# The order of three kinds of matrix product in a scheduled encoder layer: 16-bit products ahead of float32 ones, and a longer hold for the inverse steps of the early blocks

## The chip, the cores and the metric

The kernel runs on one core of a Trainium2 chip. The metric is the device time of one execution in microseconds (us); lower is better. The time before is the median of three runs, 2339.23 us (2339.19 to 2341.5).

## What is computed

One layer of a streaming encoder for 2048 frames of a new stream and 64 frames of a running one, model width 1024, all in float32:

```python
h = rmsnorm(x, norm1_w);  proj = h @ w_in          # q, k, v, z, a, b, u_pool
# (A) gated delta rule, 4 heads of 128, chunked; per chunk and head:
T = inverse(eye + Lm)                              # Lm: strictly lower triangular
u = T @ (v * beta);  w = T @ (k * beta * exp(G))
v_new = u - w @ S;  o = (q * exp(G)) @ S + qk @ v_new;  S = S * d_last + k_tail.T @ v_new
# (B) trailing means over 2/4/8/16 frames, minus the frame, one 128x128 map per group
x = x + concat(o_delta, o_pool) @ w_out
h = rmsnorm(x, norm2_w);  x = x + (silu(h @ w_gate) * (h @ w_up)) @ w_down
y = rmsnorm(x, normf_w)
```

## The kernel before, in words

**Kinds of product.** Tokens lie along the free dimension. The large products (projection `pp`, output projection `pz`, gate and up `px`/`py`/`pz`, down `d`/`dx`/`dy`/`dz`) are made of float32r products: weight and activation are each split into a high and a low part, and three products (high-high, high-low, low-high) are added in PSUM. The program calls these kind "r". Transposes and plain float32 products are kind "f": `ptk`, `ptv` (transposes of keys and values), `gr` (key and query Gram matrices), and the serial state recurrence `pk` and `po`. 16-bit products are kind "h": the triangular inverse (`py`, `pt` by level 0 to 6, then `pf` and `px_p`) and half of the decay mask (`gb`). A plain float32 product on 128 columns stands in the trace as two matmuls, a transpose and a 16-bit product as one.

**Stages.** The mixer runs over four blocks of 512 tokens (block 0 also carries the 64 frames of the running stream). For each block j: projections `pp` of one head after another (`head_project`), four heads of delta rule in the background, the pooling groups, the norm of the next block; the output projection `pz` of block j-1 stands after the second head of block j. The operand tiles h of a block have one buffer, so the next block's h can only be written once the last `pp` of this one has read them; the output projection of block 2 reads its operand from tiles in that same place, filled from DRAM (`op<-od`), after the last `pp` of block 3. The output projection of block 3 comes last, with its pooling half first and its head half second. Then the feed-forward part runs over three token blocks in Strassen form, with float32r products nearly alone.

**A delta-rule head.** Each head has two fronts of two 128-token chunks. A front goes `ptk`, `gb`, `gr`, then levels `py` (TensorE) - mask (VectorE) - `pt` (TensorE) - copy (ScalarE, `TV_p<-pt_p`) - next `py`, and so on to `pf`, `px_p`, `ptv`. The recurrence then goes chunk by chunk through `pk` and `po`, and ends in a norm (`os`), from which the head's operand of the output projection is written (`op<-osq`). Every second step of these chains is on another engine, so TensorE does other work in between.

**What sets the order.** Nothing is issued as it is written. The kernel records every operation (`Machine.note`, which is why every instruction carries line 278), and `Machine.issue` then plays the whole program through once with a cost for each operation and hands the instructions to each engine in the order that comes out. An operation has a rank: its place in the recording, less a boost. The delta-rule chains run with `BOOST` = 100000, so their ranks are negative. On the other engines the ready operation of lowest rank goes first. On TensorE, `Machine.pick` decides: if any ready product is not of kind r, the one of lowest rank is taken, unless the last product was of kind r, another r is ready, and each waiting product has been ready for less than its `HOLD`: 0.4 us of the planner's clock for negative ranks, 3.0 for others. So a run of r products is broken when one other product has waited long enough, and then all the ready others go together before the r products go on.

Of the kernel before, what the change touches and what calls it, by code (L numbers as in the profile page):

```python
# [58 lines left out]
class Machine:  # L59
# [6 lines left out]
    def __init__(self, nc):  # L66
        self.nc, self.ops, self.seen, self.boost, self.n = nc, [], {}, 0, 0
        self.tiles, self.slots, self.queue, self.parked, self.later, self.early = {}, {}, {}, {}, {}, 0
        self.free = {e: 0.0 for e in ("tensor", "vector", "scalar", "gpsimd", "sync")}
        self.last, self.at = None, 0.0  # L70
        self.busy = {"vector": 0.0, "gpsimd": 0.0}
        self.wire = 0.0
        self.gone = 0.0
        for e in self.free:
            setattr(self, e, Engine(self, e))
# [205 lines left out]
    def pick(self, ready, t):  # L281

        others = sorted(x for x in ready if x[2].kind != "r")
        if others:
            first = others[0]
            held = self.last == "r" and len(others) < len(ready) and t < min(x[2].ready + HOLD[x[0] >= 0] for x in others)
            if held:
                first = min(x for x in ready if x[2].kind == "r")
            ready.remove(first)
            heapq.heapify(ready)  # L290
            return first[2]
        return heapq.heappop(ready)[2]

    def run(self, op, t):
        op.start = t
        if op.eng == "tensor":

            free, kind = self.free["tensor"], op.kind
            if self.last == kind and op.ready <= free:
                op.start = max(t, self.at + op.ldw)  # L300
            elif kind == "r":
                if op.ready <= free:
                    op.start = max(op.ready, free - (0.028 if self.last == "h" else 0.081))
                op.occ, op.lat = op.occ + 0.087, op.lat + 0.087
            elif self.last == "h":
                op.occ, op.lat = op.occ + 0.054, op.lat + 0.054
            else:
                op.occ, op.lat = op.occ + 0.02, op.lat + 0.02
            self.at, self.last = op.start, kind
            self.free["tensor"] = op.start + op.occ  # L310
        elif op.eng == "sync":
            self.free["sync"] = t + op.occ
            self.wire = max(self.wire, t + op.occ) + op.size / (
                (STORE if op.store else 400e3) if op.size > 300000 else 320e3)
            op.lat = self.wire + 1.35 - t
        else:
            if op.port:

                other = "gpsimd" if op.eng == "vector" else "vector"
                more = min(max(self.busy[other] - t, 0.0), op.occ)  # L320
                op.occ, op.lat = op.occ + more, op.lat + more
                self.busy[op.eng] = t + op.occ
            self.free[op.eng] = t + op.occ
# [32 lines left out]
def hybrid_kernel(ctx, tc, a, o):  # L356
# [61 lines left out]
    def drain(until=lambda: False):  # L418
        while chains and not until():
            c = min((c for c in chains if c.runnable()), key=lambda c: c.at)  # L420
            if c.at > clock["pe"]:
                clock["lost"] = clock.get("lost", 0) + c.at - clock["pe"]
                clock["pe"] = c.at
            c.step()
# [93 lines left out]
    ready, due, stored = [], [], set()  # L518
# [264 lines left out]
    def project(B, *ms):  # L783

        ws = [weights("win", m) for m in ms]

        out = [[bank(("ok", (1, 2))[m][i], f"pp{m}_{i}") if B.j == 0 and m < 2 else psmm(f"pp{B.j}_{m}_{lo}")
                for i, (lo, n) in enumerate(B.subs)] for m in ms]
        for ks in (range(4), range(4, KT)) if len(ms) > 1 else (range(KT),):
            for m, w, pss in zip(ms, ws, out):  # L790
                for (lo, n), ps in zip(B.subs, pss):
                    for k in ks:
                        one_k(B, m, w[k // 4], ps[:, :n], k, slice(lo, lo + n))
                        pump()
        return out if len(ms) > 1 else out[0]
# [469 lines left out]
    def fold_pool():  # L1265

        for g in range(4):
            ts(poolw[:, g, :], poolw[:, g, :], psc[:, g : g + 1], None, ALU.mult)
            for i in range(2):
                t = wpool.tile([P, 512], F32, tag="xs", name=f"fw{g}_{i}", bufs=XBUFS["xs"])  # L1270
                sl = slice(4 * i, 4 * i + 4)
                t3 = t.rearrange("p (m c) -> p m c", c=P)
                nc.sync.dma_start(out=t3, in_=a["wout"][sl, :, (4 + g) * P : (5 + g) * P].rearrange("m p c -> p m c"))
                yield 4.0
                ps = psg(f"fp{g}_{i}")
                mm(ps, poolw[:, g, :], t, start=True, stop=True)
                nc.scalar.copy(t, ps)
                nc.sync.dma_start(out=wpd[sl, :, g * P : (g + 1) * P].rearrange("m p c -> p m c"), in_=t3)
                yield LAT_APPLY

    def new_o(B, pool=None, tag="op", bufs=2):
        four = [(pool or opool).tile([P, 4, 2, MB], F32R, tag=tag or f"h{k}", name=f"op{k}_{B.j}", bufs=bufs) for k in range(2)]
        B.o, B.o4 = [four[k // 4][:, k % 4] for k in range(KT)], four[0]

    def pools(B):
        for gs in ((0,), (1,), (2,), (3,)) if B.dec else ((0,), (1,), (2, 3)):
            pps = project(B, *(17 + g for g in gs))
            for g, pp in zip(gs, pps if len(gs) > 1 else (pps,)):
                B.pools.append(Chain(pool_group(B, g, pp)))

    def out_proj(B):
        acts = [(k, B.o[k]) for k in (4, 5, 6, 7, 0, 1, 2, 3)]

        late = [0] if B.kept else []
        src = stream_x(a["xT"], "xc", B.t0, "xc")
        for ms in ((0, 1), *((m,) for m in range(2, KT))) if B.kept else ((m,) for m in range(KT)):
            ws = [weights("wout", m, *late) for m in ms]
            for lo, n in B.subs:
                xs = [src(m, lo, n) for m in ms]
                pss = [psmm(f"pz{B.j}_{m}_{lo}") for m in ms]  # L1300
                for part in (acts[:4], acts[4:]) if len(ms) > 1 else (acts,):
                    for w, ps in zip(ws, pss):
                        dense(ps, w, part, lo, n, first=part[0] is acts[0], last=part[-1] is acts[-1])
                for m, x, ps in zip(ms, xs, pss):
                    add_x(B, m, x, ps[:, :n], lo)
# [66 lines left out]
    for j in range(NBLK):  # L1372
        first = None
        if j:
            pab, first = project(B, 0, 1)
        else:
            pab = project(B, 0)
        machine.boost = HOT_ROWS
        rows(B, pab)
        machine.boost = 0  # L1380
        blocks.append(B)
        nxt = Block(j + 1) if j + 1 < NBLK else None
        B.heads, B.pools = [], []
        if prev is None or nxt is None:
            new_o(B)
        for h in range(NH):
            B.heads += head_project(B, h, first if h == 0 else None)
            heads.append(B.heads[h])
            if h == 1 and nxt is None:
                pools(B)  # L1390
            if h == OUT_AFTER and prev is not None and nxt is not None:
                drain(lambda: all(g.done for g in prev.heads) and all(c.done for c in prev.pools))
                out_proj(prev)
                if not B.kept:
                    new_o(B)
            if h == 1 and j == 0:
                fold = Chain(fold_pool())
            if h == 1 and nxt is not None:
                norm_stats(nxt)
            if h == STATS0 and nxt is None:  # L1400
                stats0 = Chain(stats2(0, gp, "ext", 4))
        if j == 0:
            fold.wait()
        if nxt is not None:
            pools(B)
            norm_apply(nxt)
        prev, B = B, (nxt if nxt is not None else B)
# [23 lines left out]
    for k in (4, 5, 6, 7, 0, 1, 2, 3):  # L1431
        t = wpool.tile([P, 512], F32, tag="xc", name=f"od{k}", bufs=XBUFS["xc"])
# [23 lines left out]
    for nm in FH[3:]:  # L1456
        t = f2.tile([P, 4, 2, N2], F32R, tag=f"h{nm}", name=f"hB{nm}")
# [168 lines left out]
    for op in order:  # L1626
        b = op[1]
        if op[0] == "gu":
            f = op[2]
# [38 lines left out]
WSCALE, FSCALE = 2048.0, 256.0  # L1668
BOOST = 100000

HOLD = 0.4, 3.0
BACKLOG, IDLE, AHEAD_OPS = 4.0, 0.0, 400

MARGIN = {"tensor": 0.25, "vector": 0.1, "scalar": 0.1, "gpsimd": 0.1, "sync": 3.0}
# [137 lines left out]
```

## Time and profile before

| | |
|---|---|
| median of three runs | 2339.23 us (2339.19 to 2341.5) |
| the profiled execution | 2338.61 us |
| its span, first to last instruction | 2336.8 us |
| matmuls in the trace | 14614 |
| VectorE, ScalarE, GpSimd busy | 72%, 58%, 36% of the span |
| HBM read and written | 354.81 MB and 113.80 MB |

The profile is of one execution. PE is TensorE's matmuls, PEld its weight loads, DVE VectorE, ACT ScalarE, POOL GpSimd, SP the engine that issues DMAs. A row of the timeline gives the start in us from the beginning of the span, the time until the last of the group ended, the engine, the operation with its output and inputs, the tile's shape and how many instructions follow each other; matmuls overlap, so what counts is the distance between starts. Where an engine sat idle before a row, the time stands in brackets with what ended it.

### The profile page before, as it was taken

Reading aid. Unit: us, or ns where it says so; the run is one execution under the profiler, and the core shown is the slowest. Engines: PE = TensorE matmul, PEld = TensorE weight load, DVE = VectorE, ACT = ScalarE, POOL = GpSimd, SP = SyncE. Lnnn points to the kernel's source line nnn. Section 1 sums busy time; section 2 is a strip of 40 time slices with the busy share of each in tenths; the row PEclk is TensorE's granted clock in tenths of the full one; section 3 lists DMA queues with packets and bytes.
Section 4 is the critical chain, followed back from the end, with each engine's and each line's share of the span. In section 5 each row is a group of like instructions: output and inputs, shape, how many; then the busy total and the mean of one; then the engine's idle time right before and its main releaser. Section 6 shows DMA issues by size and latency. Waiting matters only on the chain.

```text
span 2336.8 us, 41455 instructions
## 1 busy us (share of the span) xinstructions
PE 2301.8 (99%) x14614; PEld 2138.4 (92%) x14614; DVE 1689.0 (72%) x3097; ACT 1356.4 (58%) x3020; POOL 843.6 (36%) x963
## 2 busy tenths in 40 slices
PE   8999999999999999999999999999999999999998
PEld 7898898778777878999999999999999999999998
DVE  8998755664676786788667665877877868766776
ACT  6987856683767675655445465554444664454444
POOL 3434222430234530554322244643432653331312
PEclk9999999999999999999999999999999999999999
DMA  8755566545464577877545377768545586455453
GB/s 293 250 160 181 169 229 209 182 156 192 165 212 159 185 206 239 294 274 252 205 169 187 139 247 231 240 205 285 181 142 183 175 289 220 146 182 189 145 193 105
DMA packets 218881, 471.36 MB, mean 202 GB/s; under 512 B 27184, under 2 KB 85552, under 8 KB 218672
## 3 DMA queue, kind: packets, MB, share of 16 engines
q1 hardware_dynamic: 218672, 468.71, 60.9%
q8 instruction: 115, 1.88, 0.3%
q14 instruction: 94, 0.77, 0.1%
HBM read 354.81 MB, written 113.80 MB: 201 GB/s over the span
## 4 chain that ended last, share of the span: by engine, by line
PE 82%; DVE 9%; ACT 4%; DMA 3%; issue 2%; POOL 0%; SPq 0%; POOLq 0%; DVEq 0%; ACTq 0%
PE px L278 19%; PE pp L278 16%; PE pz L278 12%; PE py L278 8%; PE d L278 8%; PE dx L278 6%; PE dy L278 3%; PE pk_p L278 2%; PE pt_p L278 2%; DVE hq L278 2%; PE dz L278 1%; DVE y L278 1%; PE gr_p L278 1%; PE py_p L278 1%; ACT hr L278 1%
## 5 line engine op out<-in xcount | busy, mean ns | idle before, releaser
L278 PE MATMUL pp<-h,wsp 128*128 128x512 f32 (+1 forms) x2480 | 561.0, 366 | 11.6 <-DVE wsp L278 10.3
L278 PEld LDWEIGHTS pp<-h,wsp 128*128 128x128 f32 x2480 | 400.5, 189 | 59.1 <-ACT wsp L278 8.9
L278 ACT CAST ws<-wr 128x512 fp32r<-128x512 f32 x198 | 122.0, 618 | 172.9 <-PE dx L278 49.6
L278 DVE TENSOR_TENSOR ws<-wr,ws 128x512 fp32r<-128x512 f32 x198 | 164.2, 831 | 57.3 <-ACT ws L278 51.8
L278 PE MATMUL d<-h,wsd 128*128 128x352 f32 x1056 | 170.5, 322 | 0.0
L278 PE MATMUL pz<-op,wsp 128*128 128x288 f32 (+1 forms) x768 | 169.9, 357 | 0.3 <-DVE op L278 0.2
L278 PEld LDWEIGHTS d<-h,wsd 128*128 128x128 f32 x1056 | 168.7, 188 | 0.4 <-DVE h L278 0.4
L278 ACT ACTIVATE hr<-g 128x352 f32<-128x352 f32 x132 | 65.7, 497 | 163.8 <-DVE g L278 163.5
L278 ACT CAST TV_p<-pt_p 128x512 f16<-128x512 f32 x192 | 111.1, 589 | 62.2 <-PE pt_p L278 61.7
L278 PE MATMUL px<-hA,ws 128*128 128x352 f32 x792 | 144.7, 322 | 0.7 <-DVE ws L278 0.7
L278 PE MATMUL py<-hB,wsS 128*128 128x352 f32 x792 | 143.8, 322 | 0.0
L278 PE MATMUL px<-hBT,wsS 128*128 128x352 f32 x792 | 139.6, 324 | 3.0 <-ACT g L278 2.6
L278 PE MATMUL pz<-hB,ws 128*128 128x352 f32 x792 | 142.5, 322 | 0.0
L278 PE MATMUL py<-hA,wsS 128*128 128x352 f32 x792 | 139.8, 322 | 0.0
L278 PE MATMUL px<-hBT,ws 128*128 128x352 f32 x792 | 138.1, 322 | 1.3 <-DVE u L278 1.3
L278 POOL TENSOR_TENSOR wrS<-wr,wrS 128x512 f32<-128x512 f32 x44 | 63.0, 1431 | 207.7 <-DMA wr<-in_wg_dram 64.2
L278 PE MATMUL px<-hA,wsS 128*128 128x352 f32 x792 | 137.8, 322 | 0.0
L278 PEld LDWEIGHTS px<-hBT,wsS 128*128 128x128 f32 x792 | 128.2, 188 | 7.4 <-ACT g L278 7.3
L278 PEld LDWEIGHTS px<-hA,ws 128*128 128x128 f32 x792 | 129.8, 188 | 1.2 <-DVE ws L278 1.0
L278 PEld LDWEIGHTS px<-hBT,ws 128*128 128x128 f32 x792 | 128.6, 188 | 2.3 <-DVE u L278 2.2
L278 PEld LDWEIGHTS py<-hB,wsS 128*128 128x128 f32 x792 | 129.8, 188 | 0.0
L278 PEld LDWEIGHTS pz<-hB,ws 128*128 128x128 f32 x792 | 129.6, 188 | 0.0
(686 smaller groups left out, 5606.3 us busy)
## 6 DMA issues: line engine op xcount, KB each, us to landing
wsS<-gS SPq DMA_DIRECT2D x176, 512.0 KB, 4.6
wsp<-wnd SPq DMA_DIRECT2D x126, 512.0 KB, 3.4
gS<-wsS SPq DMA_DIRECT2D x88, 512.0 KB, 4.4
wr<-in_wg_dram SPq DMA_DIRECT2D x132, 256.0 KB, 3.1
wnd<-wsp SPq DMA_DIRECT2D x42, 512.0 KB, 5.0
xd<-x2d SPq DMA_DIRECT2D x96, 176.0 KB, 3.8
wr<-in_wu_dram SPq DMA_DIRECT2D x66, 256.0 KB, 3.6
wrd<-in_wd_dram SPq DMA_DIRECT2D x56, 256.0 KB, 3.6
```

Source lines behind the costliest of these rows:

```text
L278: getattr(getattr(self.nc, op.eng), name)(*args, **kw)
```

## The change

In `pick`, the first of the ready products that are not of kind r is now chosen with the 16-bit ones ahead of the float32 ones, whatever their rank; among equals the rank decides as before. The hold becomes a function: operations of negative rank that were recorded before a mark, `calm`, may be held 0.8 instead of 0.4 us. The mark is set when the first head of the last block (j = 3, h = 0) has been recorded, so it takes in the delta-rule chains of the blocks before it. All the rest of the order follows from these two, since `issue` plays the program through again.

```diff
-        self.last, self.at = None, 0.0
+        self.last, self.at, self.calm = None, 0.0, 0
...
-            first = others[0]
-            held = self.last == "r" and len(others) < len(ready) and t < min(x[2].ready + HOLD[x[0] >= 0] for x in others)
+            first = min(others, key=lambda x: (x[2].kind == "f", x))
+            held = self.last == "r" and len(others) < len(ready) and t < min(x[2].ready + self.hold(x) for x in others)
...
+    def hold(self, x):
+
+        return HOLD[2] if x[0] < 0 and x[2].order < self.calm else HOLD[x[0] >= 0]
...
+            if (j, h) == (3, 0):
+                machine.calm = len(machine.ops)
...
-HOLD = 0.4, 3.0
+HOLD = 0.4, 3.0, 0.8
```

No instruction is added or removed on any engine. On TensorE the built order differs from the 229th product to the 6202nd of 14185 (counted as the program issues them); from there to the end, some 1306 us of the profiled span, all engines' orders are the same in both kernels. A break is a stretch of other products between two r products; a 16-bit group is a stretch of 16-bit products, which begins after an r or after an f product. Counted in the two built orders:

| TensorE's built order | before | after |
|---|---|---|
| breaks in the r products | 448 | 384 |
| 16-bit groups that begin after an r product | 273 | 309 |
| 16-bit groups that begin after an f product | 140 | 62 |
| 16-bit groups in all | 413 | 371 |
| breaks that hold f products alone | 68 | 61 |

## The prediction

> **What bounds the kernel now.** I read the page first, then the busy time by stage, then the waits of TensorE in the stage that the change reorders.
>
> ```profile
> span 2336.8 us, 41455 instructions
> PE 2301.8 (99%) x14614; PEld 2138.4 (92%) x14614; DVE 1689.0 (72%) x3097; ACT 1356.4 (58%) x3020; POOL 843.6 (36%) x963
> PE   8999999999999999999999999999999999999998
> PEclk9999999999999999999999999999999999999999
> PE 82%; DVE 9%; ACT 4%; DMA 3%; issue 2%; POOL 0%; SPq 0%; POOLq 0%; DVEq 0%; ACTq 0%
> ```
>
> TensorE is busy 99% of the span at a full granted clock, in every slice, and holds 82% of the chain that ended last. Matmuls overlap, so "busy" hides gaps of a tenth of a microsecond; those are just what this change is about. The time is the sum of TensorE's products, plus what is lost where one kind follows another, plus waits.
>
> ```profile
> 0.00:1030.00 1030.00, 1011.92 (x6627) 859.66 (x6628) 746.79 (x1508) 703.80 (x1676) 364.44 (x502) 1.00 0.64 209
> 1030.00:2336.80 1306.80, 1289.91 (x7989) 1278.79 (x7987) 942.20 (x1590) 652.59 (x1345) 479.11 (x462) 1.00 0.59 196
> ```
>
> The columns are the length and then PE, PEld, DVE, ACT and POOL busy. The orders of the two kernels part early and meet again for good at about 1030 us. The second row is then the same work in the same order, and moves as a whole. Everything is decided in the first row, where weight loads fill only 860 of 1030 us, against 1279 of 1307 in the second: there is slack between products in the mixer.
>
> ```profile
> PE pt_p L278 <- DVE Yt_p L278: 1.6, 4, 0.6
> PE pp L278 <- DVE h L278: 1.1, 2, 0.7
> PE px_p L278 <- ACT TV1F_p L278: 0.7, 2, 0.5
> PE gb_p L278 <- ACT ktl_p L278: 0.6, 1, 0.6
> PE ptv_p L278 <- DVE X_p L278: 0.5, 1, 0.5
> PE py_p L278 <- ACT TV_p L278: 0.4, 2, 0.2
> PE py_p L278 <- ACT ktl_p L278: 0.3, 1, 0.3
> ```
>
> These are TensorE's main waits from 61 to 1030 us (total us, times, longest). The six that belong to the delta-rule chains, all but the second, come to 4.1 us. That is all that better spacing of those chains can give back.
>
> **The change part by part.** No operation is added, so its cost is where it puts the products. First: what does a break cost? Three timelines of PE answer.
>
> ```profile
> 231.79 0.38 PE L278 MATMUL pk_p<-Sp,Yqk 128*128 128x128 f32 x2
> 232.01 0.39 PE L278 MATMUL po_p__864<-Qd_p,Sp 128*128 128x128 f32 x2
> 232.15 1.64 PE L278 MATMUL pp<-h,wsp 128*128 128x512 f32 x6
> 233.63 0.38 PE L278 MATMUL pk_p<-rhs_p,X_p 128*128 128x128 f32 x2
> 233.76 1.64 PE L278 MATMUL pp<-h,wsp 128*128 128x512 f32 x6
> 235.24 0.38 PE L278 MATMUL pk_p<-vn_p,ktl_p 128*128 128x128 f32 x2
> ```
>
> Two f matmuls take 0.22 us (231.79 to 232.01). From 231.79 to 233.63, 1.84 us, stand four of them (0.44) and six r; from 233.63 to 235.24, 1.61 us, two (0.22) and six r. That leaves 1.40 and 1.39 for six r, 0.232 each. I take 0.232 as the length of an undisturbed r product of 512 columns; then a break that holds f products alone costs **nothing** beyond its own products. (If r were 0.227, such a break would cost 0.03 us and each price below would be 0.03 higher.)
>
> ```profile
> 608.87 0.28 PE L278 MATMUL py_p<-id,Wh_p 128*128 128x128 f16 x2
> 608.97 1.86 PE L278 MATMUL pp<-h,wsp 128*128 128x512 f32 x7
> 610.67 0.29 PE L278 MATMUL py_p<-TV_p,Wh_p 128*128 128x128 f16 x2
> 610.77 0.94 PE L278 MATMUL pp<-h,wsp 128*128 128x512 f32 x3
> 611.55 0.29 PE L278 MATMUL py_p<-id,Wh_p 128*128 128x128 f16 x2
> ```
>
> ```profile
> 835.47 0.27 PE L278 MATMUL pt_p<-Yt_p,TV_p 128*128 128x128 f16 x2 [0.47 <-DVE Yt_p L278]
> 835.58 0.27 PE L278 MATMUL pt_p<-TV_p,Yt_p 128*128 128x128 f16 x2
> ```
>
> Two 16-bit products take 0.11 us (835.47 to 835.58). From 608.87 to 610.67, 1.80 us, stand two of them and seven r: 1.80 - 0.11 - 7 x 0.232 = 0.07. From 610.67 to 611.55, 0.88 us: 0.88 - 0.11 - 3 x 0.232 = 0.07. So a 16-bit group that begins after r costs **0.07 us**.
>
> ```profile
> 468.68 0.38 PE L278 MATMUL pk_p<-vn_p,ktl_p 128*128 128x128 f32 x2
> 468.90 0.39 PE L278 MATMUL po_p__1525<-Gam_p,vn_p 128*128 128x128 f32 x2
> 469.12 0.28 PE L278 MATMUL py_p<-TV_p,Wh_p 128*128 128x128 f16 x2
> 469.21 1.86 PE L278 MATMUL pp<-h,wsp 128*128 128x512 f32 x7
> 470.91 0.39 PE L278 MATMUL pk_p<-Sp,Yqk 128*128 128x128 f32 x2
> ```
>
> Here a 16-bit group follows f products: 2.23 us from 468.68 to 470.91, less 0.44, 0.11 and 7 x 0.232, leaves **0.056 us**. The lesson of the three: what costs is entering a 16-bit group, and where it is entered from matters little.
>
> Now the sum, with the counts of the built orders. Before: 273 x 0.07 + 140 x 0.056 = 19.1 + 7.8 = 26.9 us. After: 309 x 0.07 + 62 x 0.056 = 21.6 + 3.5 = 25.1 us. The difference is **-1.8 us**. The new rule takes away 78 groups that began after f, and pays for 36 more that begin after r. Whoever charges each of the 64 vanished breaks alike, at 0.07, gets -4.5; that is the far end, since breaks of f alone are free in the first timeline.
>
> [...]
>
> Second: what the reordering does to **waits**. A chain step needs time on another engine. In the rows above and here, the last `pt` starts at 835.64 (half of its pair's 0.11 after 835.58) and the `py` that needs its copy starts at 837.01, after waiting: about 1.4 us.
>
> ```profile
> 830.74 1.40 PE L278 MATMUL pp<-h,wsp 128*128 128x512 f32 x5
> 835.74 0.49 PE L278 MATMUL pz<-op,wsp 128*128 128x512 f32 x1
> 837.01 0.27 PE L278 MATMUL py_p<-TV_p,Wh_p 128*128 128x128 f16 x2 [0.20 <-ACT TV_p L278]
> ```
>
> With the prices above, the TensorE work between a `pt` and the `py` behind it can be summed in both built orders: the median of the 164 pairs rises from 1.68 to 2.05 us, that from `py` to `pt` from 1.68 to 1.95. So most chain steps get more cover, and some of the 4.1 us of waits should go. But a few steps get far less. At the end of block 0 (the running stream's front) one `py` follows its `pt` with 0.41 us of work between. Around the change from block 3 to the output projection of block 2, one has 0.41 and one has nothing between. I take 0 for waits, as gains and losses of like size, with -4.1 and the slow rival below as ends.
>
> Third: the **ends of the chains**. The chains are held back while r products run ahead: the last head's norm stands 53 r products ahead of the first product that reads it, where it was 81.
>
> ```profile
> 902.31 0.39 PE L278 MATMUL os_p__2856<-lo_p__2858,ones 128*128 128x512 f32 x1
> 907.96 0.68 DVE L278 TENSOR_TENSOR op<-osq_p__2855,op 128x512 fp32r<-128x512 f32 x1
> ```
>
> The operand is there 6.3 us after that norm product (902.31 to 908.64); 53 x 0.232 is 12.3. It stays covered, with 6 us to spare. The running stream's head is the tight one: 28 r of 288 columns and 11 others stand between, 5 us in all (0.13 us for such an r).
>
> ```profile
> 269.46 0.28 PE L278 MATMUL os_s<-lo_s,ones 128*128 128x256 f32 x1
> 273.18 1.31 DVE L278 TENSOR_TENSOR op<-osq_s,op 128x256 fp32r<-128x256 f32 x1
> ```
>
> It needs 5.0 us (269.46 to 274.49). That is cover used up to the last, and a late engine costs its lateness, some tenths. The DMA queue issues the same transfers in a slightly other order; weights are called for up to some 6 us earlier in block time, against a lead of three weight sets, so I count nothing.
>
> Sum: -1.8 + 0 = -1.8 us on the profiled execution, 2338.61 - 1.8 = 2336.8. That execution lies 0.6 us under the median of the runs; on the median, 2339.23 - 1.8 = **2337.4 us**.
>
> **Rivals.** *Faster: the chains' waits go too.* The longer distances remove most of the 4.1 us, and breaks cost nearer the far end of -4.5. Then -8 us: 2331. For it: the medians above, and a longer hold in three of four blocks. Against it: the breaks of f alone at 0.
>
> *Slower: no cover at the seams.* From the last `pp` (830.74 + 5 x 0.232 + 0.07, so 832.0) to the first `pz` at 835.74 there are 3.8 us without an r product, because the tiles are handed over. Before, 2.0 us of 16-bit and f products stand in that hole (`ptk` and `gr` of the next front among them); after, only eight `pt` products, 0.44 us, since the f products come later. If the hole keeps its length, TensorE loses 1.6 us more. The chain steps there and at the end of block 0, at 1.4 us per `pt`-`py` step, fall short by 1.4 + 1.0 + 0.4 at the one and 1.0 + 0.3 + 0.3 + 0.3 at the other, 4.7, and the `py`-`pt` steps by perhaps 1. With the gain: -1.8 + 1.6 + 5.7 = +5.5, so 2345. It decides once the seams cost more than 1.8 us. Against it: ScalarE has fewer copies queued ahead of the first `op<-od`, so the hole may shrink, and seams wait already today (0.47 and 0.20 in the rows above).
>
> *The change does nothing.* If the 16-bit price is a matter of the pipeline's accounting, not of time, the sum is 0: 2339.2.
>
> **How the numbers follow.** About 0.2% (4.7 us) is what a measurement of this kernel can tell from no change. Forecast, around 2337.4 and from 2335 to 2343 with partial seams: 0.60. Nothing: 0.08. Faster rival, under 2334.5: 0.20. Slower rival, over 2343.9: 0.12. So faster 0.20, same 0.68, slower 0.12. The range, 2331.5 to 2343.5, takes in the faster rival and leaves out the slower one and a tail of the faster, 0.2 in all.
>
> **What would show it.** In the profile after, the same three timelines should give 0.07, 0.056 and 0 again. The first stretch, up to the point where the orders meet, should be shorter by about 2 us, and the second equal. Chain waits between 61 and 1030 us should stay near 4 us in total, with those at the seams larger and those inside blocks smaller. I am wrong if the second stretch moves by itself, if the hole before the first `pz` costs over 3 us, or if waits for h or weights appear that are not in the rows above.

## The result, and the profile after

| | before | after |
|---|---|---|
| median, us | 2339.98 (2339.19 to 2344.61, 6 runs) | 2350.57 (2347.39 to 2351.16, 6 runs) |
| ratio, 95% interval | 1 | 1.0041 [1.0031, 1.0052] |
| the profiled execution, its span | 2338.61, 2336.8 | 2348.25, 2346.4 |

The change makes the kernel 0.41% slower, about 10 us. The forecast was 1.8 us faster, so both sign and size were missed. First lines of the page after:

```profile
span 2346.4 us, 41407 instructions
PE 2303.7 (98%) x14614; PEld 2132.7 (91%) x14614; DVE 1694.4 (72%) x3097; ACT 1352.8 (58%) x3020; POOL 851.4 (36%) x963
PE 75%; DVE 12%; ACT 7%; issue 3%; DMA 3%; POOL 1%; SPq 0%; DVEq 0%; POOLq 0%; ACTq 0%
```

The same matmuls now hold 75% of the chain that ended last, where they held 82%; VectorE and ScalarE have taken the difference. Next the busy time of each engine in the two stretches, cut 10 us later than before (columns: length; PE, PEld, DVE, ACT and POOL busy; granted clock; DMA share; GB/s):

```profile
0.00:1040.00 1040.00, 1013.78 (x6632) 854.77 (x6633) 756.21 (x1509) 699.91 (x1676) 373.69 (x502) 1.00 0.64 207
1040.00:2346.00 1306.00, 1289.94 (x7984) 1277.91 (x7982) 938.20 (x1589) 652.86 (x1345) 477.74 (x461) 1.00 0.60 196
```

The length of these rows is set by the cut, so the traces' orders decide: the last product at which the two differ starts at 1029.9 us before and at 1039.1 us after, and from there to the end it is 1306.9 and 1307.3 us. The second stretch moved as a whole, and all but a few tenths of the loss arises ahead of it. The waits of TensorE between 61 and 1040 us (total us, times, longest), the largest rows:

```profile
PE px L278 <- ACT g L278: 2.3, 3, 1.1
PE gb_p L278 <- ACT ktl_p L278: 1.8, 4, 0.7
PE pz L278 <- ACT op L278: 1.7, 2, 1.5
PE pc L278 <- DVE Rt L278: 1.4, 1, 1.4
PE py_p L278 <- ACT TV_p L278: 0.9, 2, 0.7
PE pp L278 <- ACT h L278: 0.8, 1, 0.8
PE pz L278 <- ACT wsp L278: 0.8, 1, 0.8
...
PE pz L278 <- DVE op L278: 0.6, 1, 0.6
```

Two kinds of `pz` are new in the list and a third has grown from 0.2 to 0.6 us: the output projection of block 2 waits for its operand (`op`) and its weights. `pc`, a small product of the decay factors that waits 1.4 us at 681 us, in block 3, is new too. The first row stands at the start of the feed-forward part. Was the price of switching kinds misread? Two timelines of TensorE in the kernel after, the first with breaks of f alone, the second with 16-bit groups:

```profile
241.70 0.38 PE L278 MATMUL pk_p<-rhs_p,X_p 128*128 128x128 f32 x2
241.84 2.32 PE L278 MATMUL pp<-h,wsp 128*128 128x512 f32 x9
244.00 0.39 PE L278 MATMUL pk_p<-vn_p,ktl_p 128*128 128x128 f32 x2
```

```profile
637.77 0.28 PE L278 MATMUL py_p<-TV_p,Wh_p 128*128 128x128 f16 x2
637.85 1.87 PE L278 MATMUL pp<-h,wsp 128*128 128x512 f32 x7
639.57 0.28 PE L278 MATMUL py_p<-TV_p,Wh_p 128*128 128x128 f16 x2
```

The first: 2.30 - 0.22 - 9 x 0.232 = -0.01, so free. The second: 1.80 - 0.11 - 7 x 0.232 = 0.07. Both prices stand, and by them the gain of 1.8 us; the third price, 0.056, was not read again. So some 11 us were lost on top. To place them, I took for each matmul the distance to the next start, less its own length and the price of a switch; what is left is loss, whatever its cause. By stretch of TensorE's order (the work in each is the same):

| us lost | before | after | difference |
|---|---|---|---|
| block 0 | 15.7 | 17.5 | +1.9 |
| from there to the end of block 2's projections | 5.5 | 7.0 | +1.5 |
| block 3's projections | 3.5 | 5.5 | +2.0 |
| **the seam**: last `pp` of block 3 to the third of eight `pz` tiles of block 2 | 3.6 | 8.1 | **+4.5** |
| the rest of the mixer and into the feed-forward part | 2.3 | 3.2 | +0.9 |
| feed-forward | 19.2 | 19.7 | +0.5 |
| all | 49.7 | 61.0 | +11.3 |

And -1.8 + 11.3 = 9.5, the 9.6 by which the span grew. (This agrees by construction, since the price is taken off before the loss is counted; the 1.8 us are not seen by themselves.) Here is TensorE at the seam in the kernel after: the last `pp`, the first `pz`, and the worst part.

```profile
832.11 1.86 PE L278 MATMUL pp<-h,wsp 128*128 128x512 f32 x7
...
834.68 0.51 PE L278 MATMUL pz<-op,wsp 128*128 128x512 f32 x1 [0.25 <-ACT op L278]
...
841.59 0.27 PE L278 MATMUL pt_p<-Yt_p,TV_p 128*128 128x128 f16 x2
841.70 0.27 PE L278 MATMUL pt_p<-TV_p,Yt_p 128*128 128x128 f16 x2
842.65 0.27 PE L278 MATMUL py_p<-TV_p,Wh_p 128*128 128x128 f16 x2 [0.67 <-ACT TV_p L278]
844.40 0.73 PE L278 MATMUL pz<-op,wsp 128*128 128x512 f32 x2 [1.48 <-ACT op L278]
845.22 0.38 PE L278 MATMUL ptk_p<-consts,Yqk 128*128 128x128 f32 x1
845.55 0.37 PE L278 MATMUL pt_p<-Yt_p,TV_p 128*128 128x128 f16 x2
845.72 0.42 PE L278 MATMUL pt_p<-TV_p,Yt_p 128*128 128x128 f16 x2
845.93 0.85 PE L278 MATMUL ptk_p<-consts,Yqk 128*128 128x128 f32 x3
846.43 3.18 PE L278 MATMUL pz<-op,wsp 128*128 128x512 f32 x8
849.44 0.28 PE L278 MATMUL gb_p<-Ghl,selp 128*128 128x256 f32 x1
```

Two things cost time in it. The product at 844.40 waited for ScalarE, and ScalarE's cast in turn for a load from DRAM, as its own timeline shows:

```profile
843.73 0.62 ACT L278 CAST op<-od 128x512 fp32r<-128x512 f32 x1 [1.13 <-DMA od<-od]
```

And the eight `pz` from 846.43 to 849.44 show no wait, yet take 3.01 us instead of 1.86. The busy time by stretch tells why (the column after POOL's is the granted clock):

```profile
841.96:845.37 3.41, 1.17 (x6) 0.54 (x5) 2.73 (x4) 2.23 (x5) 1.31 (x1) 1.00 1.02 379
845.37:848.78 3.41, 3.41 (x14) 2.75 (x14) 2.76 (x7) 2.81 (x14) 0.00 (x0) 0.50 0.72 233
848.78:852.19 3.41, 3.33 (x21) 2.39 (x19) 1.41 (x4) 2.43 (x11) 1.39 (x2) 1.00 0.68 208
```

TensorE was busy for 1.17 of 3.41 us, and in the next 3.41 us its clock was granted at 0.50. The work done in that stretch comes to 1.9 us undisturbed and took 1.4 us longer. The kernel before has no such stretch at the seam:

```profile
835.10:838.51 3.41, 2.75 (x20) 1.68 (x19) 3.29 (x9) 3.41 (x9) 2.48 (x3) 1.00 0.52 179
838.51:841.93 3.42, 3.40 (x26) 2.25 (x22) 3.42 (x6) 3.39 (x8) 3.11 (x3) 1.00 0.80 215
```

The page's clock line cannot show it: each of its 40 digits is a mean over 58 us, and 3.41 us at half clock leave a 9.

### The profile page after: what moved, and what is told of

Read it like the earlier page. It is cut to its first block, busy times and chain, and to the rows that moved or that the text cites. A ratio compares the mean times of both kernels' runs of the same rounds, so it can differ in the third digit from the quotient of the medians.

```text
span 2346.4 us, 41407 instructions
## 1 busy us (share of the span) xinstructions
PE 2303.7 (98%) x14614; PEld 2132.7 (91%) x14614; DVE 1694.4 (72%) x3097; ACT 1352.8 (58%) x3020; POOL 851.4 (36%) x963
## 4 chain that ended last, share of the span: by engine, by line
PE 75%; DVE 12%; ACT 7%; issue 3%; DMA 3%; POOL 1%; SPq 0%; DVEq 0%; POOLq 0%; ACTq 0%
PE px L278 17%; PE pp L278 13%; PE pz L278 11%; PE d L278 8%; PE py L278 7%; PE dx L278 5%; PE dy L278 3%; PE pk_p L278 2%; DVE hq L278 2%; DVE y L278 2%; PE pt_p L278 1%; PE dz L278 1%; ACT E L278 1%; DVE Yqk L278 1%; PE gr_p L278 1%
## 5 line engine op out<-in xcount | busy, mean ns | idle before, releaser
L278 PE MATMUL pp<-h,wsp 128*128 128x512 f32 (+1 forms) x2480 | 550.8, 364 | 11.7 <-DVE wsp L278 10.4
L278 PEld LDWEIGHTS pz<-op,wsp 128*128 128x128 f32 x768 | 120.6, 190 | 15.1 <-ACT op L278 2.3
L278 PEld LDWEIGHTS px<-hA,wsS 128*128 128x128 f32 x792 | 128.7, 188 | 3.1 <-ACT g L278 3.1
```

The costliest lines, as they stand in the source:

```text
L278: getattr(getattr(self.nc, op.eng), name)(*args, **kw)
```

## The experiments

Eight theories are named in the expectations. A: the 16-bit products, taken first, use up or displace the work that filled the seam. B: the longer hold makes the waits. C: the order before is a good draw, and almost any other order that this planner gives costs several us. D: the seam waits for the loads of the operand, which go through three buffers. A': the seam waits because its chains lack work between their steps, whatever the loads do. E: hold 0.42 was bad luck by itself. S: a store delays the loads. H: the half clock is granted on a grid in time that isn't tied to the program.

### Each half of the change alone

16-bit first, without the longer hold:

```diff
-HOLD = 0.4, 3.0, 0.8
+HOLD = 0.4, 3.0, 0.4
```

> The new choice alone, with the hold left at 0.4 us. Breaks in the built order: 438 (448 before), 16-bit groups 404 (413 before); by the prices 0.07 and 0.056 us switching is as before (27 us). Theory A (16-bit first takes the float32 filler out of the seam where block 3 hands its operand tiles to the output projection of block 2): slow, waits of over 7 us between 820 and 860 us where before has 3.6, in all about 2346. Theory B (the longer hold pushes the chains back and makes the waits): near before, 2340, seam near 3.6 us. Theory C (any other order of this schedule costs several us, since the planner's order was selected by its measured time): 2344 to 2352, with the waits somewhere.

Measured: 2345.39 us, ratio 1.0020 [1.0011, 1.0029]; 438 breaks, seam 7.7 us. The longer hold, with the old choice of the first product:

```diff
-            first = min(others, key=lambda x: (x[2].kind == "f", x))
+            first = others[0]
```

> The longer hold alone; the choice goes by rank as before. Breaks 372, 16-bit groups 378, switching 23.9 us by the prices, so 3 us less than before. Theory A: seam as before (3.6 us), time 2337 (2340 less 3). Theory B: waits 5 to 9 us above before in blocks 0 to 2, time 2343 to 2348. Theory C: 2344 to 2352.

Measured: 2343.92, ratio 1.0014 [1.0006, 1.0023]; 372 breaks, the fewest, and the cheapest switching (23.9 us); seam 8.5 us. Then 16-bit first only for the chains recorded before the mark, with the hold as in the change:

```diff
-            first = min(others, key=lambda x: (x[2].kind == "f", x))
+            first = min(others, key=lambda x: (x[2].kind == "f" and x[2].order < self.calm, x))
```

> Both parts, but 16-bit first only among operations recorded before the mark; the heads of block 3 behind it go by rank. Switching 24.4 us by the prices. Theory A: the seam's wait falls back from 8.2 to under 5 us and the time from 2350.6 to about 2346, with the other scattered waits left. Theory B: seam and time as after, within 2 us. Theory C: 2344 to 2352, without relation to the seam.

Measured: 2346.88, ratio 1.0027 [1.0016, 1.0038]; seam 5.4 us. What follows: each half alone is slower, and each alone has a slow seam, so neither A nor B by itself is the cause. (B's time came true with the hold alone, its place did not: it put the waits into blocks 0 to 2.) Block 0's loss of 17.5 us comes back in this last run (17.7), in full in neither half (15.8 and 16.5): that part needs both.

### A hold that is only nudged

The kernel before, with its one hold changed by 5%, up and then down:

```diff
-HOLD = 0.4, 3.0
+HOLD = 0.42, 3.0
```

> The kernel before with the hold of the chains at 0.42 instead of 0.40 us and nothing else: a new order with the same number of breaks (448) and switching within 0.3 us of before. Theories A and B: within 2 us of before, 2338 to 2342. Theory C: 2344 to 2352, as slow as the change, although nothing of substance was changed.

Measured: 2346.82, ratio 1.0029 [1.0018, 1.0041]; 448 breaks as before, seam 8.2 us.

```diff
-HOLD = 0.4, 3.0
+HOLD = 0.38, 3.0
```

> The kernel before with the chains' hold at 0.38 instead of 0.40 us. Switching by the prices is as before (27.0 us). Theory C (the schedule's outcome scatters by several us with any new order, and before is one of its good draws): 2342 to 2349, with a wait of 6 to 9 us at the seam between block 3 and the output projection of block 2. Theory E (the new order with a hold of 0.42 was bad luck alone, and before is a usual draw): 2338 to 2342, seam near 3.6 us.

Measured: 2348.77, ratio 1.0049 [1.0035, 1.0063]; 454 breaks, seam 8.1 us. With about as many breaks, and switching within 0.3 us of before (26.7 and 27.0), both lose most of what the change loses: 6.6 and 8.7 of its 10.6 us. This is theory C: what the change did is first of all to leave one particular order. E falls with the second nudge.

### What the seam waits for: buffers and loads

A fourth buffer for the eight operand loads, in the changed kernel:

```diff
-        t = wpool.tile([P, 512], F32, tag="xc", name=f"od{k}", bufs=XBUFS["xc"])
+        t = (gp.tile([P, 512], F32, tag="odr", name=f"od{k}", bufs=1) if k in (7, 3) else wpool.tile([P, 512], F32, tag="xc", name=f"od{k}", bufs=XBUFS["xc"]))
```

> The changed kernel, with a fourth buffer for the operand tiles that are loaded back for the output projection of block 2 (3 before), so four of the eight loads can be issued ahead of the seam instead of three. Theory D (the seam waits for these loads, which come in rounds of three): the seam's wait falls from 8.1 us by 2 to 5 us, and the time from 2350.6 to 2346 to 2349. Theory A' (the seam waits because the chains' products lack cover): seam unchanged at 8 us, time within 2 us of 2350.6.

Measured: 2344.13, ratio 1.0020 [1.0010, 1.0029]; seam 4.6 us, and no half clock in it. TensorE's order is the changed kernel's up to 841.6 us and another behind that. ScalarE's casts in this kernel:

```profile
836.10 1.68 ACT L278 CAST op<-od 128x512 fp32r<-128x512 f32 x3
844.05 1.30 ACT L278 CAST op<-od 128x512 fp32r<-128x512 f32 x2 [1.10 <-DMA od<-od]
```

Three operands are cast together where there were two, and the fifth still waits for its load, as long as the fourth did with three buffers (1.10 against 1.13 us). The same buffer in the kernel before:

> The same fourth buffer in the kernel before. Theory D: the seam's wait falls from 3.6 us to 1 to 3 us, and the time to 2338 to 2340; with theory C any reshuffle elsewhere may add up to 4 us to that. Theory A': no change at the seam.

Measured: 2339.27, ratio 1.0000 [0.9992, 1.0009]; seam 3.0 us, so little to gain there. And with the longer hold alone:

> The longer hold alone, choice by rank, with the fourth buffer. Theory D: the seam's wait falls from 8.5 to 3 to 6 us, and the time from 2343.9 to 2339 to 2342. Theory A': seam at 8 to 9 us, 2343 to 2345.

Measured: 2338.75, ratio 0.9996 [0.9987, 1.0005]; seam 5.9 us. It ties with the kernel before. No version is faster than that beyond the noise.

Then one load in place of eight, with all casts reading that one tile (seven loads of 256 KB and the right operand are left out), in the changed kernel, in the hold alone and in the kernel before. The planner plays these through anew, so their orders differ from the last part of block 3's projections on (800 to 818 us):

```diff
-        t = wpool.tile([P, 512], F32, tag="xc", name=f"od{k}", bufs=XBUFS["xc"])
-        nc.sync.dma_start(out=t, in_=od[k])
+        if k == 4:
+            t = gp.tile([P, 512], F32, tag="odr", name="od4", bufs=1)
+            nc.sync.dma_start(out=t, in_=od[k])
```

> The changed kernel with one DRAM load of the output projection's operand in place of eight: all eight casts read the one tile, so seven tiles of block 2's operand are filled with the wrong data (left out: seven loads of 256 KB). TensorE's order is the same up to block 3 and has the same products. Theory D (the seam from block 3 to the output projection of block 2 waits for those loads through three buffers): waits there fall from 8.1 us in the changed kernel to 3 or less, median about 2344 or lower. Rival A' (the chains of the delta rule lack cover there, whatever the loads do): waits at the seam stay at 4.5 to 8, median about 2346 to 2350. With four buffers it was 4.6, so between 3.5 and 4.6 both are at work.

> The longer hold alone, with the one load in place of eight as above (same work left out). With eight loads the seam waited 8.5 us, with four buffers 5.9. Theory D: 3 us or less at the seam, median about 2338 (2343.9 less 5.5). Rival A' (chains lack cover there): 5 to 6 at the seam, as with four buffers, median about 2340.

> The kernel before with the one load in place of eight (same work left out): what the seam costs without the loads. It waited 3.6 us there, 3.0 with four buffers. Theory D: 1 to 3 us, median 2337 to 2339.5. If it goes up by more than 2 us, the order that comes out of any edit is a draw by itself (theory C), and the loads explain only part.

Measured: the changed kernel 2345.81 (ratio 1.0022 [1.0014, 1.0031]), seam 4.3; the hold alone 2340.04 (0.9997 [0.9988, 1.0005]), seam 4.0; the kernel before 2343.49 (1.0011 [1.0002, 1.0019]), seam 6.3. By these totals the first two lie between what D and A' foretold. The last looks absurd: a kernel gets slower by losing seven loads. Its trace holds much of the answer, and it led to the clock: two half-clock stretches, of 6.83 us at the seam and of 3.41 us from 1004.5 us, take 3.8 of the 6.3 us by which its profiled span is longer; the kernel before has none there.

### A store ahead of the loads

In the kernel after, a store of 1536 packets of 12 bytes drains right ahead of the operand loads. I moved it to the start of the kernel (so what it stores is zeros):

```diff
     nc.vector.memset(chist, 0.0)
+    nc.sync.dma_start(out=o["cprompt"].rearrange("m p t -> p m t"), in_=chist)
...
-    for nm, t in (("cprompt", chist), ("pprompt", phist), ("csamp", shist), ("psamp", sphst)):
+    for nm, t in (("pprompt", phist), ("csamp", shist), ("psamp", sphst)):
```

> The changed kernel with the store of the convolution history (1536 packets of 12 bytes) moved to the start, right after its tile is zeroed, so that the stored history is zeros (left out: the history's last values). In the changed kernel this store drains from 834.6 to 837.4 us, right ahead of the operand loads of the seam; in the kernel before it is through by 830.6. Theory S (the store delays the loads): waits at the seam fall from 8.1 us to 5.5 or less and the median from 2350.6 to about 2347. Rival (the store is in nobody's way; the seam was as slow in two experiments whose store was through before): seam 7.5 to 8.5, median 2349 to 2351.

Measured: 2350.51, ratio 1.0039 [1.0025, 1.0052]; seam 7.0 us. The seam gave 1.1 us, block 0 lost 3.6 more at the start, where the store now stands. The cast at the seam no longer waits for its load, and the `pz` behind it waits 0.25 us instead of 1.48; half clock for 3.41 us came there all the same. So theory S, and with it that one wait for a load, is worth about 1 us, not the seam.

### Two more orders with the fourth buffer

The same buffer in hold 0.38 and in 16-bit first alone, to see whether the loads are a common cause:

> The kernel before with a hold of 0.38 and a fourth buffer for the operand loads. With three buffers the seam from block 3 to the output projection of block 2 waited 8.1 us and the median was 2348.8. Theory D as a common cause: seam 4 to 5.5 us, median about 2345. Rival (the loads cost only in the changed kernel; the spread of the orders comes from chains without cover): seam 7 to 8.5, median 2347 or more.

> 16-bit first alone (hold 0.4 throughout) with a fourth buffer. With three buffers the seam waited 7.7 us and the median was 2345.4. Theory D as a common cause: seam 4 to 5.5 us, median about 2342. Rival: seam 7 or more, median 2344 to 2346.

Measured: hold 0.38 with four buffers 2348.62 (1.0035 [1.0021, 1.0049]), seam 8.7; 16-bit first with four buffers 2340.02 (0.9999 [0.9990, 1.0008]), seam 2.9. By these totals one order does better than D foretold, and the other does not follow it at all. The profile of the first has 10.24 us at half clock at the seam:

```profile
836.40:839.81 3.41, 1.97 (x17) 1.30 (x16) 1.45 (x5) 3.41 (x17) 0.92 (x1) 1.00 0.90 141
839.81:850.05 10.24, 8.19 (x32) 5.22 (x32) 6.19 (x17) 7.92 (x23) 3.88 (x5) 0.50 0.52 115
```

### The same kernels once more

Three kernels were run again with no edit: the changed one, the hold alone, and hold 0.38 with four buffers.

> The changed kernel, unchanged, profiled once more. Its first profile has one stretch of 3.41 us at half clock, 845.4 to 848.8, in which 1.9 us worth of products took 1.4 us longer. Theory H (the clock is granted by a grid of 3.41 us that runs free of the program): the order and the waits for other engines are the same, but the stretch begins elsewhere by up to 3.4 us, or there are none or two; the seam's total of 8.1 us becomes 6.5 to 10, with 1.4 us for each stretch. Rival (the stretch belongs to the order): one of 3.41 us again within half a microsecond of 845.4, seam 8.1 within 0.3.

> The longer hold alone, unchanged, profiled once more. First profile: half clock from 829.8 to 833.2 and from 840.1 to 843.5, seam 8.5 us, span 2340.2; timed runs 2340.9 to 2345.4. Theory H: other stretches, none to three, and the span moves with them by about 1.4 us each. Rival: the same two.

> Hold 0.38 with four buffers, unchanged, profiled once more. First profile: half clock from 225.4 to 228.8 and for three windows from 839.8 to 850.1, seam 8.7 us, span 2348.1. Theory H: fewer windows are as likely, and each that is gone takes about 1.1 to 1.5 us off the seam; without any it would be 5.3 us. Rival: the same three, seam 8.7 within 0.3.

Measured: the changed kernel 2348.91 (1.0038 [1.0018, 1.0057]), with 6.83 us at half clock in place of 3.41, and begun 1.5 us earlier:

```profile
840.43:843.85 3.42, 1.54 (x10) 0.83 (x8) 1.66 (x4) 0.58 (x1) 0.09 (x1) 1.00 0.95 284
843.85:847.26 3.41, 2.56 (x11) 1.96 (x12) 3.41 (x6) 3.22 (x8) 1.22 (x1) 0.50 0.60 210
847.26:850.67 3.41, 3.41 (x10) 2.63 (x10) 1.32 (x4) 1.35 (x9) 0.00 (x0) 0.50 0.93 253
```

Its seam is 9.5 us, where it was 8.1. The hold alone, 2343.79 (1.0019 [1.0007, 1.0030]), shows the same two stretches again, 0.15 us earlier. Hold 0.38 with four buffers, 2348.27 (1.0037 [1.0018, 1.0057]), has its three windows at the seam again, 1.3 us earlier, while the window that it had at 225.4 us is gone, and its span is 2345.7 instead of 2348.1 us. So H is borne out by two of three; the third fits the rival too, since it can have met the grid at the same point. The other profiles decide it: in all seven that hold two such stretches, their starts lie whole multiples of 3.413 us apart (3 twice, 46, 49, 179, 180 and 241 of them; 3.413 is the length that the trace of the changed kernel gives its stretch), while the same kernel's stretches begin at other times in another run. So in these profiles the stretches lie on a grid, and the order of the program didn't set where it lay.

With that the seams can be read without the clock. The clock's part is, for each matmul in such a stretch, what it took over its own length, at most that length again (in the changed kernel's stretch `pz` products stood 0.43 us apart, against 0.227 at full clock):

| us at the seam | lost | at half clock | of it the clock's | the rest |
|---|---|---|---|---|
| before / four buffers / one load | 3.6 / 3.0 / 6.3 | 0 / 0 / 6.83 | 0 / 0 / 2.4 | 3.6 / 3.0 / 3.9 |
| after | 8.1, 9.5 again | 3.41, 6.83 | 1.4, 2.6 | 6.7, 6.8 |
| after, four buffers / one load | 4.6 / 4.3 | 0 / 3.41 | 0 / 1.4 | 4.6 / 3.0 |
| hold alone, again | 8.6 | 2 x 3.41 | 2.8 | 5.8 |
| hold, four buffers / one load | 5.9 / 4.0 | 3.41 / 3.41 | 1.3 / 1.3 | 4.6 / 2.6 |
| 16-bit first / four buffers | 7.7 / 2.9 | 3.41 / 0 | 1.4 / 0 | 6.3 / 2.9 |
| hold 0.42 | 8.2 | 0 | 0 | 8.2 |
| hold 0.38 / four buffers | 8.1 / 8.7, 8.8 again | 6.83 / 10.24 twice | 2.4 / 3.4, 3.9 | 5.7 / 5.3, 4.9 |

The last column is steady where the totals were not: 6.7 and 6.8 in two runs of the changed kernel, and 2.6 to 3.9 in all three orders without the loads. Without them, or with a fourth buffer, it falls by 2.1 and 3.7 us in the changed kernel, by 1.2 and 3.2 with the hold alone and by 3.4 in 16-bit first, and hardly in the kernel before. That speaks for D in these three orders. It isn't shown cleanly, because each of these edits also makes another order at the seam, and waits for a load as such are few in the traces: one of 1.13 us in the changed kernel, none with the hold alone. The loads may act through the order that the planner makes for them; no run separates the two. In hold 0.38 the fourth buffer takes off only 0.4 to 0.8, so there chains without cover (A') weigh more. And hold 0.42 loses 8.2 us at the seam without any half clock, so a seam can be slow without the clock, which comes on top.

## Why the prediction was wrong

**What bounds the kernel.** Right: TensorE bounds it, the second stretch moved as a whole, everything was decided ahead of it. Of the clock, "full in every slice" was true of the slices, and of the kernel before until its last matmul ended at 2328.5 us (0.50 was granted from 2330.1 us to its end), and I took it as given for any order. It wasn't: behind the new waits at the seam the clock was granted at 0.50 for 3.41 us, and for 6.83 in the second profile of the same kernel.

**The prices.** With the 0.232 us that the prediction takes for an undisturbed r product, 0 and 0.07 were read in both kernels. But 0.232 was taken from runs of six r products between breaks, so it holds part of the break. The kernel before has a run of 192 r products of 512 columns (`pz<-op,wsl`, from 902.54 to 946.10 us, 0.227 each), and in long runs of `pp` they stand 0.227 apart as well (77 of them from 360.01 us, 73 from 581.58 us). So the prediction's bracket applies: a break of f alone costs some 0.03 us and is not free, and the other prices are 0.03 higher. Its counts then give 41.4 us before and 38.1 after, -3.3 instead of -1.8, and the loss on top is some 13 us instead of 11.3.

**Waits.** Here it failed: "I take 0 for waits, as gains and losses of like size". What TensorE loses grew by 11.3 us, 1.4 of it by the clock. The waits of the chains' own products, small rows included, rose from 4.3 to 6.2 us where the prediction said near 4. I argued from the median distance between chain steps, which did rise; but where a median step was covered already, more cover gave nothing here, and the few steps without cover paid. All that could be won was 4.1 us, as I had quoted; what could be lost had no such bound, and I gave both like size. One of the prediction's own signs of being wrong appeared too: waits for h (0.8 us) and for weights (0.8 us).

**The slower rival** named two places and a size for each. The seam: 1.6 for the hole and 2.8 for the chain steps, 4.4 together, against +4.5 measured. The place is right, the mechanism is not: the hole before the first `pz` shrank from 3.8 to 0.9 us (832.11 + 7 x 0.232 + 0.07 is 833.8, and the first `pz` starts at 834.68), and the loss came 8 to 15 us later. Of the 4.5 us, 1.4 are the clock's and 3.1 are other loss; with one load in place of eight they are gone, together with the order that had them. The end of block 0: 1.9 forecast, and block 0 did lose 1.9 more, but elsewhere. Between 1.5 and 2 us of it are there already at 140 us, among them a wait of 0.68 us of `ptk_p` at 90 us. Around the running stream's steps, from 205 to 240 us, TensorE's waits come to 1.4 us in both kernels. So one size met the right place by another mechanism, and the other is a coincidence. What the rival left out is the rest, +4.9 us over blocks 1 to 3 and the feed-forward part. With it 2345 becomes 2350. And its chance, 0.12, was too small for what stood behind it: its two places were counted in the built order, while for the forecast's zero stood only a median. The range had a slip of its own: it begins at 2331.5 and is said to take in the faster rival, whose time is 2331.

**Ends of the chains.** "I count nothing" for the DMA queue was a smaller part of the failed step: the loads of `od` are called for when a buffer comes free, and one of them landed so late that ScalarE's cast waited 1.13 us for it and the seam's longest wait, 1.48 us, stood behind that cast. In the kernel before no cast waited for a load.

**What stays open.** Why blocks 1 to 3 lose 3.5 us more was not taken apart; the wait of 1.4 us of `pc` in block 3 is the largest single piece (the changed kernel with one load has it too, at 681.2 us, and half clock for 3.41 us behind it). How the loads come to cost what they do at the seam is open as said above. That nearly every other order is slower (six of six with the loads as they were, by 3.7 to 10.6 us) is shown; with a fourth buffer three of five orders tie with the kernel before; that the order before is good because its hold was chosen for it is only the likely reading.

## What to carry to other kernels

Where one engine is busy 99% and an order decides the rest, price a reordering by its worst places, not by the median: here cover that was already enough gained nothing, and the chains' waits rose from 4.3 to 6.2 us while the median work between their steps rose. Nudge the planner's constant by a few per cent first; if both neighbours lose most of what the change loses, the order is a draw, and the change must be judged over several of them, or with the weak place mended (here one more buffer took 6.4 us off the changed kernel, 4.8 off its second measurement, and nothing clear of noise off the one before). And look for the clock in windows of a few us around a new wait, since slices of 58 us showed nothing of 3.41 us at 0.50.

## What the runs showed of the hardware

**Half clock came behind short waits.** Before 1030 us, half clock (0.50 granted) came in stretches of 3.41, 6.83 or 10.24 us, in 13 of the 17 experiments' profiles (in 12 of them in the mixer) and in the changed kernel's; each stretch began behind 3.41 us in which TensorE was between 29 and 67% busy (34% in the changed kernel). Such windows also passed without it. The first pair of rows is from the hold alone, the second from hold 0.42, where no half clock came:

```profile
826.40:829.82 3.42, 2.11 (x16) 1.22 (x15) 3.38 (x6) 3.39 (x8) 0.93 (x1) 1.00 0.36 43
829.82:833.23 3.41, 3.41 (x14) 2.28 (x15) 3.41 (x8) 3.00 (x7) 0.41 (x1) 0.50 1.03 340
```

```profile
838.98:842.40 3.42, 1.53 (x10) 1.13 (x11) 2.84 (x8) 2.03 (x5) 0.67 (x1) 1.00 0.77 207
842.40:845.81 3.41, 3.02 (x24) 1.70 (x22) 3.41 (x9) 3.35 (x7) 3.14 (x3) 1.00 0.74 211
```

62% busy was followed by half clock, 45% was not; busy time of matmuls alone doesn't decide it. The longest single wait before the changed kernel's stretch was 1.48 us, in a window 34% busy, and with one load in place of eight it was 0.70 us, in a window 64% busy. So waits of 0.7 to 1.5 us among shorter ones stood ahead of it in these two; what else it takes is not shown.

**The DMA engines were busy at a low rate.** Around the store of 18 KB in 1536 packets of 12 bytes, which drained from 834.6 to 837.4 us in the kernel after, the busy share was full and the rate a little over a third of that in the next 5 us:

```profile
835.00:840.00 5.00, 4.16 (x26) 2.90 (x26) 4.96 (x9) 4.97 (x11) 0.35 (x1) 1.00 1.10 99
840.00:845.00 5.00, 2.73 (x16) 1.67 (x15) 3.86 (x6) 2.28 (x5) 1.31 (x1) 1.00 0.91 271
```

The store is not all of it. Half a microsecond behind its last packet the rate is still low:

```profile
838.00:838.50 0.50, 0.50 (x3) 0.38 (x3) 0.50 (x2) 0.50 (x2) 0.00 (x0) 1.00 1.04 80
```

What holds it down there is not shown; with the store moved away, the seam gained about 1 us.
